# Attention's values: plain products first, and the other weight sums grown in four raw pages

## The chip, the cores and the metric

The kernel runs on one core of a Trainium2 chip. Its engines work side by side, each through its own instructions in order: TensorE (PE; its weight loads are PEld), VectorE (DVE), ScalarE (ACT), GpSimd (POOL) and SyncE (SP). Transfers run on 16 DMA engines that the core shares among its queues: SP and ACT issue plain transfers, POOL issues those that add to their destination, and some stores. The metric is the time of one execution on the device in microseconds (us).

## The reference, cut to what matters

One layer of a hybrid encoder for 512 tokens, model width 2048, in float32. The part that counts here is the first projection and its split:

```python
h = rms_norm(x, norm_mix_w[i])
proj = h @ w_in[i]
q_a, k_a, v_a, q_g, k_g, v_g, r_g, gate_lr = split_cols(proj, IN_SPLITS)
...
gate_logit = (gate_lr @ w_gla_gate_up[i] + b_gla_gate[i]).astype(jnp.float32)
log_a = (jax.nn.log_sigmoid(gate_logit) / GLA_GATE_TAU).reshape(B, T, GLA_HEADS, GLA_DK)
```

`v_a` (attention's values) and `v_g` (the values of gated linear attention) are 1024 columns each. The gate's logarithm is summed up along each chunk of 64 tokens (a scan) and used as exp(b) and exp(-b). Attention, gated linear attention, the output projection, a gated feed-forward block and a gated embedding follow.

## The kernel before, in words

Every product of matrices is made of float32r pieces: a weight page of 128 x 1024 is loaded raw, ACT copies it to a high part, VectorE subtracts that from the raw page and gives the low part ("split"), and three products of halves are added in PSUM. Each half has a ring of three buffers (tags h0 to h2 and l0 to l2), so the split of page n + 2 waits until PE has ended page n - 1.

The work goes in this order: `first_values` and `second_values` make the two halves of `v_g` with plain products, eight pages of 24 matmuls each; then comes attention's values; then the list of steps of all later projections, beginning with q and k of the four linear heads (units 12 to 15).

Attention's values are the product of two matrices cut in two both ways, with seven products of quarters in place of eight. The weights' quarters are L11, L12, L21 and L22, and the products P1 to P7 want L11, L12, S1 = L21 + L22, S2 = S1 + L11, S3 = L21 + L11, S4 = S2 + L12 and L22. The operand's quarters are R11, R21 and R22 and the differences N1, N2, T3 and T4. Each product takes four pages of 12 matmuls (128 x 512), so there are 28 pages, numbered 0 to 27 in the order of `VALUE_ORDER`. `values_product` loads page n + 4, splits page n + 2, runs what `plan` holds for page n and then gives page n to PE. `values_collect` brings a finished product from PSUM into one of four result quarters C11, C12, C21 and C22 (`VALUE_SLOTS`, halves of the x pages) and stores a finished quarter to DRAM (`vad`, L1173).

The sums of weights are made beforehand in DRAM: `value_chores` copies a page from DRAM to DRAM on SP's queue (L1113) and two chores later adds another to it on POOL's (L1116), for four pages of each of S1, S2, S4 and S3. The chores run between the pages of the gated values.

The x pages hold the layer's input in eight pairs of blocks (tags r3 to r7, u0, u1 and c0). `scale_pair(k)` applies the norm to pair k and makes R11's piece, `right(k)` makes those of R21 and R22, `differences(k)` replaces the pair by its four differences (four instructions of VectorE) and `spread_differences(k)` splits these into operand pieces named "h" (one instruction of ACT and one of VectorE). Pairs 2 to 7 get their differences between pages 4 and 14. The gate's steps are `gate_low` to `gate_ln`, `gate_sum`, `gate_scan`, `gate_decay` and `gate_small`; sums and scans run in the last pages of `second_values`.

`values_out` evicts a half of `v_g` from PSUM on ACT and stores it to DRAM (`vgd`, L277) from ACT's queue. `linear` loads it again (`load_v`, L1374, SP).

What sets the order: a scheduler may move instructions, except where an `InOrder` engine (`vec`, `act`, `ten`, `syn`) is switched on by `in_order`. From `second_values` on, ACT, VectorE and TensorE keep the order of the program text; SP does not, and POOL has no such wrapper. `give(tag)` returns a tag to the list of free pages and lets `issue` load weights of the coming steps into it.

## Time and profile before

| what | value |
|---|---|
| median of three runs | 2264.49 us (2262.75 to 2265.28) |
| the profiled execution's own time | 2269.32 us |
| its span | 2267.4 us |
| granted clock of TensorE over it | 0.995 |
| first matmul of attention's values | 104.36 us |
| first matmul of the steps after them | 199.65 us |

The profile is of one execution. Times in its views count from the start of the span. A row of the timeline has start, length, engine, line, operation and tiles, and in brackets the idle time of the engine ahead of it and what ended it; nearly all instructions stand under L64, the wrapper's line, so that they are told apart by their tiles: "wva_P_r" is a raw page of attention's values, "wva_h" and "wva_l" its halves, "vaA", "vaB" and "vaC" the PSUM banks, "h" the spread differences, "va_S" a sum in DRAM, "g_t" a tile of the gated part. A row of a group has its count, busy time and mean length; a row of waits has us in total, times and the longest. A row of stretches has the length, busy time and count for each engine, the granted clock, the DMA engines' share and GB/s.

### The profile page before, as it was taken

What the parts mean: (1) busy time and instruction counts of PE and PEld (TensorE: products, weight loads), DVE (VectorE), ACT (ScalarE), POOL (GpSimd) and SP (SyncE); (2) the same over time, 40 slices, a digit from 0 to 9 for tenths busy, and PEclk for the clock granted to TensorE, in tenths of its full rate; (3) what the DMA queues carried; (4) which work ended last, traced back from release to release, by engine and by line L of the source; (5) the groups of instructions that cost most, each with busy time, mean ns of one, the idle gap of its engine ahead of it and who ended that gap; (6) DMA issues with size and microseconds to landing.
All of it is one profiled execution on the core that took longest, in us unless ns stands there. A gap on an engine that the chain in (4) does not pass through costs nothing.

```text
span 2267.4 us, 45711 instructions
## 1 busy us (share of the span) xinstructions
PE 2240.1 (99%) x18248; PEld 2182.5 (96%) x18248; DVE 1893.6 (84%) x2599; ACT 1322.3 (58%) x1960; POOL 198.6 (9%) x243
## 2 busy tenths in 40 slices
PE   9989999999999999999999999999999999999997
PEld 8768999999999999999999999999999999999997
DVE  5775779998788888999888888888898787898987
ACT  6564567776575665555555555555564554666765
POOL 1101111010000001111111110000000100000000
PEclk9999999999999999999999999999999999999999
DMA  9967888887978979999999987877866967879896
GB/s 295 303 228 205 224 230 231 234 241 215 335 280 256 327 240 257 290 291 289 283 271 275 271 231 210 219 214 202 249 237 227 306 217 227 324 243 333 282 294 207
DMA packets 205830, 583.42 MB, mean 257 GB/s; under 512 B 22480, under 2 KB 64720, under 8 KB 205616
## 3 DMA queue, kind: packets, MB, share of 16 engines
q1 hardware_dynamic: 169680, 460.12, 56.9%
q0 software_dynamic: 32320, 115.88, 27.4%
q10 hardware_dynamic: 3616, 4.49, 0.6%
q8 instruction: 143, 2.34, 0.4%
q14 instruction: 71, 0.58, 0.1%
HBM read 507.01 MB, written 136.31 MB: 284 GB/s over the span
## 4 chain that ended last, share of the span: by engine, by line
PE 85%; DVE 6%; DMA 5%; ACT 2%; issue 2%; ACTq 0%; SPq 0%; DVEq 0%; POOLq 0%
PE accA L64 42%; PE accC L64 22%; PE accB L64 11%; PE v L64 3%; DVE wl L64 1%; PE vaA L64 1%; DMA on<-ond 1%; PE pp L64 1%; PE psc L64 1%; PE ptr L64 1%; PE py L64 1%; DMA wva_P_r<-in_w_v_a 1%; DMA s<-in_w_up 1%; DVE u L64 1%; DVE s L64 1%
## 5 line engine op out<-in xcount | busy, mean ns | idle before, releaser
L64 DVE TENSOR_TENSOR wl<-s,wh 128x1024 fp32r<-128x1024 f32 (+1 forms) x381 | 457.6, 1201 | 82.3 <-ACT wh L64 76.8
L64 ACT ACTIVATE wh<-l 128x1024 fp32r<-128x1024 f32 (+1 forms) x320 | 331.7, 1038 | 187.0 <-PE accC L64 119.4
L64 PE MATMUL accA<-h,wh 128*128 128x256 f32 x3392 | 433.8, 280 | 0.6 <-ACT u L64 0.5
L64 DVE TENSOR_TENSOR wl<-l,wh 128x1024 fp32r<-128x1024 f32 (+1 forms) x320 | 382.5, 1196 | 59.4 <-ACT wh L64 58.7
L64 ACT ACTIVATE wh<-s 128x1024 fp32r<-128x1024 f32 (+1 forms) x381 | 395.0, 1037 | 38.1 <-DVE s L64 21.7
L64 PEld LDWEIGHTS accA<-h,wh 128*128 128x128 f32 x3392 | 412.4, 188 | 3.2 <-ACT u L64 1.2
L64 PE MATMUL accC<-h,wh 128*128 128x256 f32 x2832 | 361.5, 279 | 0.3 <-ACT u L64 0.3
L64 PEld LDWEIGHTS accC<-h,wh 128*128 128x128 f32 x2832 | 343.8, 188 | 0.8 <-ACT u L64 0.5
L64 ACT ACTIVATE u<-accA 128x256 f32<-128x256 f32 x302 | 114.2, 378 | 381.5 <-PE accA L64 381.3
L64 PE MATMUL accA<-h,wl 128*128 128x256 f32 x1696 | 233.5, 279 | 0.7 <-DVE wl L64 0.7
L64 DVE TENSOR_TENSOR s<-s,l 128x1024 f32<-128x1024 f32 (+1 forms) x176 | 211.3, 1201 | 7.7 <-DMA s<-in_w_blk 4.2
L64 PEld LDWEIGHTS accA<-h,wl 128*128 128x128 f32 x1696 | 213.4, 188 | 0.9 <-DVE wl L64 0.9
L64 PE MATMUL accC<-h,wl 128*128 128x256 f32 x1416 | 195.2, 279 | 0.9 <-DVE wl L64 0.9
L64 PEld LDWEIGHTS accC<-h,wl 128*128 128x128 f32 x1416 | 178.3, 188 | 1.3 <-DVE wl L64 1.3
L442 POOL DMA_DIRECT2D s<-in_w_up x84 | 74.0, 880 | 738.5 <-DMA s<-in_w_up 284.1
L64 DVE SCALAR_TENSOR_TENSOR cv<-u,cw,cv 128x511 f32<-128x511 f32 (+1 forms) x176 | 131.7, 748 | 3.1
L64 ACT ACTIVATE u<-accC 128x256 f32<-128x256 f32 x98 | 37.4, 382 | 91.1 <-PE accC L64 90.7
L64 DVE TENSOR_TENSOR u<-u,accC 128x256 f32<-128x256 f32 x102 | 42.7, 418 | 56.8 <-PE accC L64 55.7
L64 PE MATMUL accA<-up_N,wh 128*128 128x256 f32 x704 | 89.5, 279 | 0.4 <-ACT u L64 0.4
L64 PE MATMUL accA<-up_R,wh 128*128 128x256 f32 x704 | 89.7, 280 | 0.0
L64 PE MATMUL accB<-up_R,wh 128*128 128x256 f32 x704 | 89.3, 279 | 0.0
L64 PEld LDWEIGHTS accA<-up_N,wh 128*128 128x128 f32 x704 | 85.2, 188 | 0.6 <-ACT u L64 0.6
(343 smaller groups left out, 3649.8 us busy)
## 6 DMA issues: line engine op xcount, KB each, us to landing
l<-in_w_up SPq DMA_DIRECT2D x132, 512.0 KB, 6.7
s<-in_w_up SPq DMA_DIRECT2D x84, 512.0 KB, 6.0
s<-in_w_up POOLq DMA_DIRECT2D x84, 512.0 KB, 7.6
l<-in_w_dn SPq DMA_DIRECT2D x56, 448.0 KB, 4.9
l<-in_w_blk SPq DMA_DIRECT2D x48, 512.0 KB, 5.3
s<-in_w_blk SPq DMA_DIRECT2D x32, 512.0 KB, 4.5
s<-in_w_blk POOLq DMA_DIRECT2D x32, 512.0 KB, 7.3
l<-in_w_out SPq DMA_DIRECT2D x28, 512.0 KB, 4.7
```

Of the source, the lines that this page charges most:

```text
L64: ins = f(*args, **kw)
L442: nc.gpsimd.dma_start(t, src("L22" if name == "S1" else "L11"), accum_op=ALU.add)
```

## The change

The sums are no longer made in DRAM: `value_chores` and its calls are gone. The products go in the order P1, P2, P4, P5, P6, P3, P7: first the three with plain weights. In the meantime four raw pages (tags r4, r5, r7 and u0) are loaded with L21 and get L22 added to them (S1, for P5); when a page has been split, L11 is added (S2, for P6), and after the next split L12 (S4, for P3). P7's four pages are loaded with L21 on the ordinary ring and get L11 added. All of these adds are accumulating DMAs from POOL into SBUF, tied to page numbers.

The operand work moves with it. Pairs 0 to 3 get their differences and spreads within `second_values` and pair 4 its differences there, the rest by page 9. Gate sums and scans move from `second_values` to pages 10 to 15, decays to 16 to 19. The second half of `v_g` is evicted in pages 0 and 1 instead of ahead of them. The stores of `v_g` move from ACT's queue to POOL's, and POOL gets a wrapper of its own; SP and POOL keep the order of the text within the stage. The vgd loads in `load_v` keep it too. C11 and C12 use one pair of result halves (slot 3), C22 and C21 slots 6 and 7; a fourth bank D is used; and P7 ends two quarters, C21 and C22.

```diff
-    def values_out(ps, c, tiles):
-        for t in range(TT):
+    def values_out(ps, c, tiles, ts=range(TT)):
+        for t in ts:
             act.activation(tiles[t], ps[t], AF.Copy, scale=rtok[:, t:t + 1])
-            nc.scalar.dma_start(vgd[2 * c:2 * c + 2, :, t].rearrange("h p v -> p h v"),
+            pool.dma_start(vgd[2 * c:2 * c + 2, :, t].rearrange("h p v -> p h v"),
...
-    VALUE_SLOTS = {"C11": 1, "C12": 4, "C22": 5, "C21": 7}
-    VALUE_ORDER = ("P1", "P2", "P3", "P6", "P5", "P7", "P4")
-    VALUE_BANKS = {"P1": "A", "P2": "B", "P3": "C", "P6": "A", "P5": "B", "P7": "A", "P4": "A"}
+    VALUE_SLOTS = {"C11": 3, "C12": 3, "C22": 6, "C21": 7}
+    VALUE_ORDER = ("P1", "P2", "P4", "P5", "P6", "P3", "P7")
+    VALUE_BANKS = {"P1": "A", "P2": "B", "P4": "D", "P5": "C", "P6": "A", "P3": "C", "P7": "A"}
+    SUM_TAGS = ("r4", "r5", "r7", "u0")
...
     def value_load(v, n):
-        if n < len(v["pages"]):
-            prod, j = v["pages"][n]
-            raw = v["raw"][n] = page("wr", f"wva_{prod}{j}_r")
-            syn.dma_start(raw, value_page(PRODUCTS[prod][0], j))
+        prod, j = v["pages"][n]
+        raw = v["raw"][n] = page("wr", f"wva_{prod}{j}_r")
+        syn.dma_start(raw, value_page("L21" if prod == "P7" else PRODUCTS[prod][0], j))
+
+    def sum_load(v, j):
+        raw = v["sum"][j] = pg.tile([P, 1024], F32, tag=SUM_TAGS[j], name=f"wva_s{j}")
+        syn.dma_start(raw, value_page("L21", j))
+
+    def sum_more(v, n, name):
+        prod, j = v["pages"][n]
+        raw = v["raw"][n] if prod == "P7" else v["sum"][j]
+        v["raw"][n] = raw
+        pool.dma_start(raw, value_page(name, j), accum_op=ALU.add)
...
-        todo = {0: [(gate_low,), (scale_pair, 2)],
-                1: [(scale_pair, 3), (right, 0), (right, 1)],
+        todo = {0: [(gate_low,), (scale_pair, 2), (right, 0)],
+                1: [(scale_pair, 3), (differences, 0), (right, 1)],
                 2: [(gate_up,), (gate_abs, (0, 1)), (scale_pair, 4), (gate_min, (0, 1))],
                 3: [(gate_abs, (2, 3)), (scale_pair, 5), (gate_min, (2, 3)), (right, 2)],
-                4: [(gate_exp, (0, 1, 2, 3)), (scale_pair, 6), (differences, 0)],
-                5: [(gate_ln, (0, 1, 2, 3)), (scale_pair, 7), (gate_sum, (0, 1))],
-                6: [(gate_sum, (2, 3)), (gate_scan, (0, 1))],
-                7: [(gate_scan, (2, 3)), (spread_differences, 0)]}
+                4: [(gate_exp, (0, 1, 2, 3)), (scale_pair, 6), (differences, 1), (right, 3)],
+                5: [(gate_ln, (0, 1, 2, 3)), (scale_pair, 7), (differences, 2)],
+                6: [(spread_differences, 0), (differences, 3), (spread_differences, 1)],
+                7: [(spread_differences, 2), (spread_differences, 3), (right, 4), (differences, 4)]}
...
+    for n, *fs in ((0, (second_out, (0, 1)), (spread_differences, 4)),
+                   (1, (second_out, (2, 3)), (sum_load, va, 0), (right, 5), (right, 6)), (2, (differences, 5)),
+                   (3, (sum_load, va, 1), (spread_differences, 5)), (4, (right, 7), (sum_more, va, 12, "L22")),
+                   (5, (sum_load, va, 2), (differences, 6)), (6, (sum_more, va, 13, "L22"), (spread_differences, 6)),
+                   (7, (sum_load, va, 3), (differences, 7)), (8, (sum_more, va, 14, "L22")),
+                   (9, (sum_more, va, 15, "L22"), (spread_differences, 7)), (10, (gate_sum, (0, 1))), (11, (gate_scan, (0,))),
+                   (12, (gate_sum, (2, 3))), (13, (gate_scan, (1,))), (14, (gate_scan, (2,))), (15, (gate_scan, (3,))),
+                   *((11 + j, (sum_more, va, 16 + j, "L11"), (value_load, va, 24 + j)) for j in range(4)),
+                   *((15 + j, (sum_more, va, 20 + j, "L12")) for j in range(4)),
+                   *((18 + j, (sum_more, va, 24 + j, "L11")) for j in range(4)),
+                   *((16 + i, (gate_decay, (i,))) for i in range(4)),
+                   *((20 + i, (gate_small, (i,))) for i in range(4)), (26, (linear_pages,)),
+                   *((n, (give, tag)) for n, tag in ((19, "r4"), (20, "r5"), (23, "r1"), (24, "r2"), (25, "r0"), (26, "r3")))):
```

More of the change, by code (lines that the diff above doesn't have):

```diff
@@ L70, in encoder_block @@
     vec, act, ten = InOrder(nc.vector), InOrder(nc.scalar), InOrder(nc.tensor)
-    syn = InOrder(nc.sync)
+    syn, pool = InOrder(nc.sync), InOrder(nc.gpsimd)
     def in_order(on, loads=False):
@@ L76, in in_order @@
             e.on = on
-        syn.on = loads
+        syn.on = pool.on = loads
     ident = cp.tile([P, P], F32, name="ident")
@@ L247, in first_values @@
             if kp == 4:
-                chores.extend(value_chores())
                 gate_weights()
@@ L436, in issue @@
             if name[0] == "L":
-                nc.sync.dma_start(t, src(name))
+                syn.dma_start(t, src(name))
             elif unit.sums == "memory":
@@ L440, in issue @@
             else:
-                nc.sync.dma_start(t, src("L21"))
-                nc.gpsimd.dma_start(t, src("L22" if name == "S1" else "L11"), accum_op=ALU.add)
+                syn.dma_start(t, src("L21"))
+                pool.dma_start(t, src("L22" if name == "S1" else "L11"), accum_op=ALU.add)
     sumd = {}
@@ L1095, in norm_root @@
         norm["w"] = rstd_begin(norm["ms"])
-    value_sums, plan = {}, {}
+    plan = {}
+    VALUE_SLOTS = {"C11": 3, "C12": 3, "C22": 6, "C21": 7}
+    VALUE_ORDER = ("P1", "P2", "P4", "P5", "P6", "P3", "P7")
+    VALUE_BANKS = {"P1": "A", "P2": "B", "P4": "D", "P5": "C", "P6": "A", "P3": "C", "P7": "A"}
+    SUM_TAGS = ("r4", "r5", "r7", "u0")
     def value_page(name, j):
-        if name[0] == "S":
-            return value_sums[name, j]
         return A["w_v_a"][int(name[1]) - 1, 4 * (int(name[2]) - 1) + j]
-    def value_chores():
-        todo = [(name, j) for name in ("S1", "S2", "S4", "S3") for j in range(4)]
-        first = {"S1": "L21", "S2": "L11", "S3": "L21", "S4": "L12"}
-        second = {"S1": "L22", "S2": "S1", "S3": "L11", "S4": "S2"}
-        def chore(i):
-            if i < len(todo):
-                name, j = todo[i]
-                value_sums[name, j] = scratch(f"va_{name}{j}", (P, 1152))[:, :1024]
-                tc.keep_in_program_order(nc.sync.dma_start(value_sums[name, j], value_page(first[name], j)))
-            if 2 <= i < len(todo) + 2:
-                name, j = todo[i - 2]
-                tc.keep_in_program_order(nc.gpsimd.dma_start(value_sums[name, j], value_page(second[name], j),
-                                                             accum_op=ALU.add))
-        return [lambda i=i: chore(i) for i in range(len(todo) + 2)]
@@ L1139, in values_product @@
         acc2 = v["ps"][VALUE_BANKS[prod]]
-        fresh = prod in ("P1", "P2", "P3", "P5")
+        fresh = prod in ("P1", "P2", "P4", "P5")
         for j in range(4):
             n = 4 * VALUE_ORDER.index(prod) + j
-            value_load(v, n + 4)
+            if n + 4 < 12:
+                value_load(v, n + 4)
             value_split(v, n + 2)
@@ L1161, in values_collect @@
         acc2 = v["ps"][VALUE_BANKS[prod]]
-        parts = {"P1": (("C11", 1, 0),), "P2": (("C11", 1, 1),), "P3": (("C12", 1, 0),), "P6": (("C12", 1, 0),),
-                 "P5": (("C22", -1, 0), ("C12", 1, 1)), "P7": (("C22", -1, 1),), "P4": (("C21", -1, 1),)}[prod]
+        parts = {"P1": (("C11", 1, 0),), "P2": (("C11", 1, 1),), "P4": (("C21", -1, 0),), "P5": (("C22", -1, 0),),
+                 "P6": (("C12", 1, 0),), "P3": (("C12", 1, 1),), "P7": (("C21", -1, 1), ("C22", -1, 1))}[prod]
         for quarter, sign, done in parts:
@@ L1172, in values_collect @@
                 if done:
-                    nc.gpsimd.dma_start(vad[4 * c:4 * c + 4, :, 2 * h + i].rearrange("b p v -> p b v"),
+                    pool.dma_start(vad[4 * c:4 * c + 4, :, 2 * h + i].rearrange("b p v -> p b v"),
                                         dst.rearrange("p (b v) -> p b v", b=4))
@@ L1330, in split_page @@
                 value_split(va, k - KD // 2)
-            for _ in range(2 if 2 <= k < 6 else 1):
-                if chores:
-                    chores.pop(0)()
-        todo = {0: [(gate_low,), (scale_pair, 2)],
-                1: [(scale_pair, 3), (right, 0), (right, 1)],
+        todo = {0: [(gate_low,), (scale_pair, 2), (right, 0)],
+                1: [(scale_pair, 3), (differences, 0), (right, 1)],
                 2: [(gate_up,), (gate_abs, (0, 1)), (scale_pair, 4), (gate_min, (0, 1))],
                 3: [(gate_abs, (2, 3)), (scale_pair, 5), (gate_min, (2, 3)), (right, 2)],
-                4: [(gate_exp, (0, 1, 2, 3)), (scale_pair, 6), (differences, 0)],
-                5: [(gate_ln, (0, 1, 2, 3)), (scale_pair, 7), (gate_sum, (0, 1))],
-                6: [(gate_sum, (2, 3)), (gate_scan, (0, 1))],
-                7: [(gate_scan, (2, 3)), (spread_differences, 0)]}
+                4: [(gate_exp, (0, 1, 2, 3)), (scale_pair, 6), (differences, 1), (right, 3)],
+                5: [(gate_ln, (0, 1, 2, 3)), (scale_pair, 7), (differences, 2)],
+                6: [(spread_differences, 0), (differences, 3), (spread_differences, 1)],
+                7: [(spread_differences, 2), (spread_differences, 3), (right, 4), (differences, 4)]}
         for k in range(3):
@@ L1358, in second_values @@
             values_page(ps, *tiles.pop(k), k)
-        values_out(ps, 1, [gt("t8"), gt("t9"), gt("S", 768)[:, :T], gt("t10")])
+        va["first"] = ps
     def linear(unit):
@@ L1373, in load_v @@
             for i in range(2):
-                nc.sync.dma_start(M["V"][i], vgd[h][:, 2 * i:2 * i + 2])
+                tc.keep_in_program_order(nc.sync.dma_start(M["V"][i], vgd[h][:, 2 * i:2 * i + 2]))
         def keys():
@@ L1488, in linear_pages @@
         G["s"] = pg.tile([P, 2, T], F32R, tag="r7", name="squares")
+    va = dict(pages=[(p, j) for p in VALUE_ORDER for j in range(4)], raw={}, sum={}, tiles={}, have=set())
     def at_page(n, *fs):
@@ L1495, in give @@
         issue()
-    for n, *fs in ((0, (differences, 1)), (1, (spread_differences, 1)), (2, (right, 3), (right, 4)), (3, (right, 5), (right, 6)),
-                   (4, (right, 7)), *((4 + 2 * i - (i == 5), (differences, 2 + i)) for i in range(6)),
-                   *((5 + 2 * i - (i == 5), (spread_differences, 2 + i)) for i in range(6)),
-                   *((3 + 2 * i, (gate_decay, (i,))) for i in range(4)),
-                   *((15 + i, (gate_small, (i,))) for i in range(4)), (24, (linear_pages,)),
-                   *((n, (give, tag)) for n, tag in ((16, "r5"), (18, "r4"), (23, "r1"), (24, "r2"), (25, "r0"), (26, "r3")))):
+    out_tiles = []
@@ new lines, in second_out @@
+    def second_out(ts):
+        if not out_tiles:
+            out_tiles.extend((gt("t8"), gt("t9"), gt("S", 768)[:, :T], tp.tile([P, T], F32, tag="sq", name="v_out")))
+        values_out(va["first"], 1, out_tiles, ts)
+    for n, *fs in ((0, (second_out, (0, 1)), (spread_differences, 4)),
[11 more added lines that the diff above has]
+                   *((n, (give, tag)) for n, tag in ((19, "r4"), (20, "r5"), (23, "r1"), (24, "r2"), (25, "r0"), (26, "r3")))):
@@ L1503, in encoder_block @@
         at_page(n, *(lambda f=f, a=a: f(*a) for f, *a in fs))
-    va = dict(pages=[(p, j) for p in VALUE_ORDER for j in range(4)], raw={}, tiles={}, have=set())
     first_values(A["w_v_g"])
     second_values(A["w_v_g"])
-    va["ps"] = {b: [(psum_mm if b == "C" else psum_aux)(f"va{b}{i}") for i in range(2)] for b in "ABC"}
+    in_order(True, True)
+    va["ps"] = {b: [(psum_mm if b in "CD" else psum_aux)(f"va{b}{i}") for i in range(2)] for b in "ABDC"}
     for p in VALUE_ORDER:
         values_product(va, p)
-        if p == "P4":
+        if p == VALUE_ORDER[-1]:
@@ L1514, in encoder_block @@
         values_collect(va, p)
+    in_order(True)
     pctx.close()
```

## The prediction

> **What bounds the kernel now.** I read the page first, for the kernel as a whole.

> ```profile
> span 2267.4 us, 45711 instructions
> PE 2240.1 (99%) x18248; PEld 2182.5 (96%) x18248; DVE 1893.6 (84%) x2599; ACT 1322.3 (58%) x1960; POOL 198.6 (9%) x243
> q1 hardware_dynamic: 169680, 460.12, 56.9%
> q0 software_dynamic: 32320, 115.88, 27.4%
> ```

> TensorE is busy nearly throughout, so only a stage in which it waits, or runs below its clock, can pay. The second reading is busy time by stage: the second half of the gated values (59.86 to 104.36), attention's values (104.36 to 199.65, the stage of this change), the first products after it; and two short stretches inside the stage.

> ```profile
> 59.86:104.36 44.50, 44.50 (x197) 36.79 (x196) 32.49 (x48) 23.40 (x35) 7.31 (x9) 1.00 1.04 309
> 104.36:199.65 95.29, 86.69 (x337) 65.00 (x336) 68.02 (x93) 51.90 (x66) 7.83 (x10) 0.95 0.74 227
> 110.00:118.00 8.00, 5.49 (x14) 3.38 (x13) 3.50 (x6) 2.81 (x3) 0.00 (x0) 0.79 0.89 282
> 162.00:168.00 6.00, 6.00 (x15) 4.69 (x16) 3.98 (x10) 1.06 (x1) 0.00 (x0) 0.52 0.64 188
> 199.65:220.00 20.35, 20.35 (x176) 20.34 (x175) 9.66 (x11) 9.22 (x13) 3.31 (x4) 1.00 0.79 230
> ```

> The columns are length, then PE, PEld, DVE, ACT and POOL busy, the granted clock, the DMA engines' share and GB/s. Before and after the stage PE is full at clock 1.00. Inside it is idle 95.29 - 86.69 = 8.6 us, at a mean clock of 0.95; the loss of clock sits behind the stalls (0.79 in 110 to 118, 0.52 in 162 to 168). VectorE has 68 of 95 us, so it is no bound over the stage as a whole.

> Third, the pitch of an undisturbed page: the eviction of each page's high part starts when a page of products has ended, so two neighbours at the end of the stage show it.

> ```profile
> 179.72 1.06 ACT L64 ACTIVATE wva_h<-wva_P_r 128x1024 fp32r<-128x1024 f32 x1 [1.25 <-PE vaA L64]
> 182.52 1.06 ACT L64 ACTIVATE wva_h<-wva_P_r 128x1024 fp32r<-128x1024 f32 x1 [1.74 <-PE vaA L64]
> ```

> 182.52 - 179.72 = 2.80 us a page; 28 pages need 78.4 us. The stage takes 95.29, so **16.9 us** is all there is to win in it: 8.6 idle, the rest lost clock and short gaps.

> Fourth, who ends PE's waits in the stage.

> ```profile
> PE vaA L64 <- DVE h L64: 2.7, 2, 2.2
> PE vaA L64 <- DVE wva_l L64: 1.9, 3, 0.8
> PE vaA L64 <- ACT wva_h L64: 1.6, 2, 1.1
> PE vaB L64 <- DVE wva_l L64: 1.1, 2, 0.8
> PE vaC L64 <- DVE wva_l L64: 0.9, 2, 0.5
> ```

> Two causes stand behind these rows. The weight pages came late, and ACT, in order, was late behind them; and the operand pieces that VectorE spreads ("h") came one by one between the pages' own splits, the last at 160.50, with PE standing for it.

> ```profile
> ACT wva_h L64 <- DMA wva_P_r<-in_w_v_a: 14.5, 3, 5.6
> 96.98 1.06 ACT L64 ACTIVATE wva_h<-wva_P_r 128x1024 fp32r<-128x1024 f32 x1 [3.87 <-DMA wva_P_r<-in_w_v_a]
> 103.61 1.06 ACT L64 ACTIVATE wva_h<-wva_P_r 128x1024 fp32r<-128x1024 f32 x1 [5.57 <-DMA wva_P_r<-in_w_v_a]
> 106.23 0.37 ACTq L277 DMA_DIRECT2D vgd<-g_t  x1
> SPq L1374 <- DMA vgd<-g_t: 8.0, 2, 7.1
> 159.50 0.73 PE L64 MATMUL vaA<-wva_h,h 128*128 128x512 f32 x2 [2.15 <-DVE h L64]
> 160.50 1.22 DVE L64 TENSOR_TENSOR h<-pair_c,h 128x1024 fp32r<-128x1024 f32 x1
> ```

> **The change, part by part.** Write T(n) for the start of page n; T(0) = 104.36, pages 2.80 apart if nothing stalls. Durations, back to back, from groups of the stage and single rows:

> ```profile
> L64 DVE TENSOR_TENSOR wva_l<-wva_P_r,wva_h 128x1024 fp32r<-128x1024 f32 x27 | 33.0, 1223 | 25.2 <-ACT wva_h L64 25.2
> L64 ACT ACTIVATE wva_h<-wva_P_r 128x1024 fp32r<-128x1024 f32 x27 | 28.0, 1053 | 30.4 <-DMA wva_P_r<-in_w_v_a 10.6 <-PE vaA L64 8.7 <-PE vaB L64 7.0
> 112.34 0.88 DVE L64 TENSOR_TENSOR pair_r<-pair_r 128x256 f32<-128x256 f32 x2
> 113.26 0.88 DVE L64 SCALAR_TENSOR_TENSOR pair_r<-pair_r 128x256 f32<-128x256 f32 x2
> 100.42 2.33 DVE L64 TENSOR_TENSOR_SCAN g_t<-g_t,g_t 128x512 f32<-128x512 f32 x2
> 93.49 1.29 DVE L64 TENSOR_TENSOR g_t<-g_t,g_t 128x512 f32<-128x512 f32 x2
> 120.74 1.29 DVE L64 TENSOR_TENSOR in_R<-pair_r,in_R 128x512 fp32r<-128x512 f32 x2
> L64 DVE TENSOR_TENSOR pair_r<-pair_r,vaB 128x512 f32<-128x512 f32 x4 | 2.7, 684 | 0.4 <-ACT pair_u L64 0.4
> 105.53 0.67 ACT L64 ACTIVATE g_t<-v,rtok 128x512 f32<-128x512 f32 x1
> 106.64 0.69 ACT L64 ACTIVATE g_t<-v,rtok 128x512 f32<-128x512 f32 x1 [0.44 <-ACT g_t L64]
> ```

> So a split costs ACT 1.05 and VectorE 1.22; differences 2 x 0.88 = 1.76; a scan 1.17; a gate sum or a "right" piece 0.65; an add of results 0.68; a spread piece as much as a split.

> *Sums out of DRAM.* 16 DRAM-to-DRAM copies (SP) and 16 DRAM accumulates (POOL) go, and of 28 page loads 12 plain ones, four sum loads and four for P7 stay: 24 fewer issues on SP. POOL keeps 16 accumulates, now into SBUF and between the page's uses. This frees the DMA engines before T(0), where their share is 1.04: the pages that ACT got at 96.98 and 103.61 were issued at 79.75 and 85.19, 17 and 18 us before; at the pace of the stage a load takes 4.2. I cost the loads of P1, P2 and P4 at nothing, behind two pages of lead.

> ```profile
> 79.75 0.33 SPq L64 DMA_DIRECT2D wva_P_r<-in_w_v_a  x1
> 85.19 0.33 SPq L64 DMA_DIRECT2D wva_P_r<-in_w_v_a  x1
> wva_P_r<-in_w_v_a SPq DMA_DIRECT2D x8, 512.0 KB, 4.2
> L442 POOL DMA_DIRECT2D s<-in_w_blk x32: 851/877/1418, 189.0 to 575.4; - x32
> DMA to landing us min/median/max: 5.1/7.8/15.4
> 196.49 1.22 DVE L64 TENSOR_TENSOR s<-s,l 128x1024 f32<-128x1024 f32 x1
> ```

> *Stores.* The four stores of the second half of gated values stood on ACT's queue between evictions; from one eviction to the next went 106.64 - 105.53 = 1.1 us, and 0.67 without the store; all eight go to POOL (0.88 us an issue), on which nothing else waits then. The evictions themselves now follow the splits of pages 2 and 3 instead of going ahead of page 2's. The vgd loads of the first linear unit leave SP's queue in the stage, where SP stood 8.0 us for them; they now follow in their place, as the later units' do.

> *Differences and spreads earlier.* Four differences (7.0), four spreads (4.9) and two "right" pieces (1.4) now lie ahead of T(0), two scans (2.3) and four sums (2.6) leave. VectorE there: 32.5 + 13.3 - 4.9 + the second page's split 1.2 = 42.1 of 44.5 us. It fits; only the last of the eight pages (about 6 us against 5.5) runs over. In the stage VectorE has 28 splits (34.2), four spreads (4.9), three differences (5.3), three "right" (2.0), sums and scans (2.6 + 4.7), small decays and four adds of results (4.3): 58 of 78.4. Page by page the sums are at most 2.9 us of 2.8 (pages 2, 5, 7), and neighbours are lighter. A page's high part may start two pages before its use, at T(n), and both halves are done by T(n) + 2.3; they are wanted at T(n) + 5.6, so 3.3 us of queueing are free. Put down in their order, ACT and VectorE come closest at page 6, where a late spread and P1's two copies hold ACT to T(4) + 1.7 (both halves done at + 3.9, wanted at + 5.6), and at page 10, where P2's two adds hold VectorE to T(8) + 2.8 (done at + 4.0). At least 1.6 us are left, so the cost is zero; without that cover each page would stall by what it lacks.

> *The four growing pages.* This is the unknown price. Page 12 + j is split by T(10+j) + 2.3; then its accumulate may issue, lands L later, and page 16 + j needs 2.3 more and is wanted at T(16+j). So L may be 16.8 - 4.6 = 12.2 us. L of all such accumulates is 5.1 / 7.8 / 15.4 (smallest, median, largest), so at the median 4.4 us remain. On POOL's queue the accumulates for pages 14 and 15 stand behind the stores of C11, which wait for VectorE's adds after T(8); they issue near T(8) + 3.5 and 4.3, 11 and 13 us before their splits must begin (T(14) - 2.3 and T(15) - 2.3): more than 7.8.

> The DMA engines bound L. From the page, a 0.524 MB accumulate holds all 16 for 0.524 / (115.88 / (0.274 x 2267.4)) = 2.8 us, a load 0.524 / (460.12 / (0.569 x 2267.4)) = 1.5. Between T(8) and T(24), 44.8 us, stand 14 accumulates (39.3), four loads (5.9) and two 256 KB stores (2.8): 48.0, and at the share of 1.04 that the row before the stage reached, 46.6 fit. The engines are then full, 1.4 to 3.2 us over. Nothing (the 4.4 us cover it) and 6.4 (3.2 idle, and as much again at half clock) are the ends of the bill; I take 2.0 (1.0 idle, 1.0 of clock), nearer nothing, because the last four (P7's) were never urgent: issued from about T(17) + 3, wanted from T(22).

> *The end of the stage.* P7 ends with four adds on VectorE (2.7 us) instead of two ACT copies; the next split that PE wants is due at T(28) + 5.6. The first linear unit's S1 page comes free at T(22) + 2.3, loads (4.2) and accumulates (7.8): T(22) + 14.3, and its sum (1.22) and split (2.3) must be begun by T(28) + 2.1 = T(22) + 18.9. Covered by 4.6; without that cover PE would wait for the rest in the first product that uses it.

> *Sum.* Profiled time 2269.3 (span 2267.4) - 16.9 + 2.0 = 2254.4. The median of the runs, 2264.5, lies 4.8 under that execution, so 2249.6.

> *The clock.* The rows of 110 to 118 have PE idle for 2.5 us in gaps of at most 1.1 us, and a clock of 0.79; so I let a stall cost its length again. [...]

> **The rivals.**
> *Faster, but the chain of sums is late.* L near 12 to 14 while loads of the next stage share the engines; PE then waits at P6, P3 or P7. For it: the engines are full. Against: the stage's own loads are over by then. Price 5 to 11 in place of 2.0: 2252.6 to 2258.6.
> *Slower.* One mechanism, the sums' loop. If L stays at 15.4 or more, page 16 waits 15.4 - 12.2 = 3.2, and in P3, whose pages now start late, each round takes 15.4 + 2.3 instead of 11.2, 6.5 more: 9.7 idle, and with half clock after each of the two (162 to 168, at 0.52, loses 2.9 us) 15.5, nearly all of the gain of 16.9. Beyond about 16 it is slower: at 18, 5.8 + 9.1 + 5.8 = 20.7, 2268.3. Against: 15.4 is the largest that this line shows.
> *No change.* The stalls were the split order's, not the loads', and come back at pages 0 to 3, where ACT has over 3 us a page (split, two evictions, a spread) and VectorE enters late: 1 us a page over the first 14 and clock loss, about 2264.

> **How the numbers follow.** As forecast 0.62 (2245.5 to 2254.5), late chain 0.20, no change 0.06, slower 0.12. A measurement of this kernel can tell about 0.2%, 4.5 us. Faster 0.82, same 0.06, slower 0.12. The range 2245.5 to 2262 leaves out the slower case and little else.

> **What would show it.** Right: no wait of PE for "h" or "wva_h" in the stage, granted clock 1.00 from 104 on, the stage near 80 us, evictions 2.80 apart, wva pages landed in 4 to 6 us. The price of the chain: PE or ACT waiting for the DMA into "wva_s", and the landing times of POOL's accumulates against 12.2. Wrong: gaps that begin at page 16 and repeat every four pages, a granted clock of a half behind them, or a first product after the stage that waits for its S1.

## The result and the profile after

The changed kernel takes 2252.22 us (median of 4 runs, 2250.46 to 2254.96), the kernel before 2264.89 beside it: a ratio of 0.9941, 95% interval 0.9920 to 0.9963. Two later series of 5 runs each gave 2254.17 and 2252.47, with the kernel before at 2264.96 and 2264.35 (ratios 0.9955 and 0.9946). It is 11 to 13 us faster; 15 were forecast. The profiled execution took 2254.96 (span 2253.2); the sum had 2254.4 for it.

The page of the kernel after:

```profile
span 2253.2 us, 45669 instructions
PE 2230.6 (99%) x18248; PEld 2178.5 (97%) x18248; DVE 1892.1 (84%) x2599; ACT 1321.7 (59%) x1960; POOL 205.8 (9%) x251
q1 hardware_dynamic: 166224, 447.54, 55.7%
q0 software_dynamic: 32960, 117.98, 27.5%
```

Busy time by stage (length, PE, PEld, DVE, ACT, POOL, granted clock, DMA share, GB/s), with the second half of the gated values, attention's values and the first steps after them:

```profile
59.50:104.00 44.50, 44.50 (x198) 36.79 (x197) 37.80 (x59) 27.80 (x40) 0.00 (x0) 1.00 0.31 108
104.00:184.56 80.56, 79.46 (x337) 62.88 (x336) 56.28 (x75) 47.25 (x60) 21.98 (x26) 1.00 0.98 254
184.56:220.00 35.44, 31.94 (x272) 31.31 (x271) 24.81 (x29) 13.79 (x18) 5.32 (x7) 1.00 0.89 257
```

The stage went from 95.29 to 80.56 us, at full clock. Ahead of it the DMA engines' share fell from 1.04 to 0.31; now the stage itself has them full, at 0.98. The third row is new: PE stands 3.5 us *after* the stage, where before it lost 0.2. Who ended PE's waits from 104 to 220, and ACT's from 104 to 200:

```profile
PE accB L64 <- DVE wl L64: 1.8, 1, 1.8
PE pat L64 <- DVE g_t L64: 1.7, 1, 1.7
PE vaA L64 <- DVE wva_l L64: 0.8, 1, 0.8
PE vaA L64 <- ACT wva_h L64: 0.2, 1, 0.2
```

```profile
ACT wva_h L64 <- DMA wva_P_r<-in_w_v_a: 17.3, 6, 4.1
ACT wva_h L64 <- DMA wva_s<-in_w_v_a: 7.0, 5, 1.9
```

No wait for "h" is left, and the products ahead of P7 cost PE nothing: all their pages, and P7's first, start 2.80 us after the one before. The two small waits in the stage stand at P7's pages (174.3 and 175.6), the last three of which come 3.1, 3.9 and 3.1 us after the one before. ACT's timeline there (start, length, operation, idle time ahead and its releaser) shows them as they land:

```profile
161.90 2.14 ACT L64 ACTIVATE wva_h<-wva_s 128x1024 fp32r<-128x1024 f32 x2
168.15 1.06 ACT L64 ACTIVATE wva_h<-wva_P_r 128x1024 fp32r<-128x1024 f32 x1 [4.10 <-DMA wva_P_r<-in_w_v_a]
173.22 1.06 ACT L64 ACTIVATE wva_h<-wva_P_r 128x1024 fp32r<-128x1024 f32 x1 [4.01 <-DMA wva_P_r<-in_w_v_a]
176.36 1.06 ACT L64 ACTIVATE wva_h<-wva_P_r 128x1024 fp32r<-128x1024 f32 x1 [2.08 <-DMA wva_P_r<-in_w_v_a]
179.52 1.06 ACT L64 ACTIVATE wva_h<-wva_P_r 128x1024 fp32r<-128x1024 f32 x1 [2.10 <-DMA wva_P_r<-in_w_v_a]
```

Their four accumulates were issued from 157.4 to 159.0, so they took 10.7 to 20.4 us to land, twice as long as the twelve into the growing pages (groups of DMA issues from 104 to 200: count, KB each, median us to landing):

```profile
wva_s<-in_w_v_a POOLq DMA_DIRECT2D x12, 512.0 KB, 8.3
wva_P_r<-in_w_v_a POOLq DMA_DIRECT2D x4, 512.0 KB, 16.5
```

The late pages also explain the waits after the stage. The first linear unit's S1 page is the page that P7's first split frees (170.47). From there the timeline of SP, POOL and VectorE runs so:

```profile
170.49 5.40 SPq L64 DMA_DIRECT2D s<-in_w_blk  x2
178.72 0.86 POOL L64 DMA_DIRECT2D s<-in_w_blk  x1 [17.48 <-DVE wva_l L64]
185.63 1.23 DVE L64 TENSOR_TENSOR s<-s,l 128x1024 f32<-128x1024 f32 x1 [2.65 <-DMA s<-in_w_blk]
208.39 1.23 DVE L64 TENSOR_TENSOR s<-s,l 128x1024 f32<-128x1024 f32 x1 [6.40 <-DMA s<-in_w_blk]
```

S1 is complete at 185.6. PE still bridges that, but this unit's pages come free late, so the next unit's S1 lands at 208.3, and VectorE, in order, stands 6.4 us for it with two low parts and the gate's work queued behind: those are PE's waits of 1.8 and 1.7.

### The profile page after: what moved, and what is told of

Read it like the earlier page. It is cut to its first block, busy times and chain, and to the rows that moved or that the text cites. A ratio compares the mean times of both kernels' runs of the same rounds, so it can differ in the third digit from the quotient of the medians.

```text
span 2253.2 us, 45669 instructions
## 1 busy us (share of the span) xinstructions
PE 2230.6 (99%) x18248; PEld 2178.5 (97%) x18248; DVE 1892.1 (84%) x2599; ACT 1321.7 (59%) x1960; POOL 205.8 (9%) x251
## 4 chain that ended last, share of the span: by engine, by line
PE 82%; DVE 4%; DMA 2%; ACT 1%; issue 1%; DVEq 0%; SPq 0%; ACTq 0%
PE accA L64 44%; PE accC L64 22%; PE accB L64 11%; DVE wl L64 1%; PE pp L64 1%; PE py L64 1%; PE psc L64 1%; PE ptr L64 1%; DVE u L64 1%; PE po L64 1%; DVE s L64 1%; DVE xs L64 0%; DMA on<-ond 0%; DMA x3d<-xs 0%; DMA s<-in_w_ple_gate 0%
## 5 line engine op out<-in xcount | busy, mean ns | idle before, releaser
L64 DVE TENSOR_TENSOR wl<-s,wh 128x1024 fp32r<-128x1024 f32 (+1 forms) x381 | 457.4, 1201 | 77.3 <-ACT wh L64 70.2
L64 ACT ACTIVATE wh<-l 128x1024 fp32r<-128x1024 f32 (+1 forms) x320 | 331.7, 1038 | 183.2 <-PE accC L64 119.1
L64 PE MATMUL accA<-h,wh 128*128 128x256 f32 x3392 | 433.7, 280 | 0.6 <-ACT u L64 0.5
L64 DVE TENSOR_TENSOR wl<-l,wh 128x1024 fp32r<-128x1024 f32 (+1 forms) x320 | 382.5, 1195 | 57.2 <-ACT wh L64 56.4
L64 ACT ACTIVATE wh<-s 128x1024 fp32r<-128x1024 f32 (+1 forms) x381 | 394.7, 1036 | 42.3 <-DVE s L64 27.5
L64 PEld LDWEIGHTS accA<-h,wh 128*128 128x128 f32 x3392 | 411.8, 188 | 3.2 <-ACT u L64 1.2
L64 PE MATMUL accC<-h,wh 128*128 128x256 f32 x2832 | 361.4, 280 | 0.5 <-ACT u L64 0.5
L64 PEld LDWEIGHTS accC<-h,wh 128*128 128x128 f32 x2832 | 343.2, 188 | 0.9 <-ACT u L64 0.7
L64 ACT ACTIVATE u<-accA 128x256 f32<-128x256 f32 x302 | 114.3, 379 | 382.1 <-PE accA L64 381.9
L64 PE MATMUL accA<-h,wl 128*128 128x256 f32 x1696 | 233.5, 279 | 0.7 <-DVE wl L64 0.7
L64 DVE TENSOR_TENSOR s<-s,l 128x1024 f32<-128x1024 f32 (+1 forms) x176 | 211.2, 1200 | 10.2 <-DMA s<-in_w_blk 10.2
L64 PEld LDWEIGHTS accA<-h,wl 128*128 128x128 f32 x1696 | 213.0, 188 | 0.9 <-DVE wl L64 0.9
L64 PE MATMUL accC<-h,wl 128*128 128x256 f32 x1416 | 195.0, 279 | 0.3 <-DVE wl L64 0.3
L64 PEld LDWEIGHTS accC<-h,wl 128*128 128x128 f32 x1416 | 177.8, 188 | 0.5 <-DVE wl L64 0.5
L64 POOL DMA_DIRECT2D s<-in_w_up x84 | 74.0, 881 | 734.5 <-DMA s<-in_w_up 393.0
L64 DVE SCALAR_TENSOR_TENSOR cv<-u,cw,cv 128x511 f32<-128x511 f32 (+1 forms) x176 | 131.6, 748 | 3.1
L64 DVE TENSOR_TENSOR u<-u,accC 128x256 f32<-128x256 f32 x102 | 42.6, 418 | 57.9 <-PE accC L64 57.0
L64 ACT ACTIVATE u<-accC 128x256 f32<-128x256 f32 x98 | 37.4, 382 | 91.3 <-PE accC L64 90.9
L64 PE MATMUL accA<-up_R,wh 128*128 128x256 f32 x704 | 89.8, 280 | 0.0
L64 PE MATMUL accB<-up_R,wh 128*128 128x256 f32 x704 | 89.4, 279 | 0.0
L64 PE MATMUL accA<-up_N,wh 128*128 128x256 f32 x704 | 89.4, 279 | 0.0
L64 PEld LDWEIGHTS accA<-up_R,wh 128*128 128x128 f32 x704 | 85.2, 188 | 0.5 <-issue 0.5
## 6 DMA issues: line engine op xcount, KB each, us to landing
l<-in_w_up SPq DMA_DIRECT2D x132, 512.0 KB, 6.5
s<-in_w_up SPq DMA_DIRECT2D x84, 512.0 KB, 5.9
s<-in_w_up POOLq DMA_DIRECT2D x84, 512.0 KB, 7.6
l<-in_w_blk SPq DMA_DIRECT2D x48, 512.0 KB, 5.5
s<-in_w_blk SPq DMA_DIRECT2D x32, 512.0 KB, 4.7
s<-in_w_blk POOLq DMA_DIRECT2D x32, 512.0 KB, 7.8
l<-in_w_out SPq DMA_DIRECT2D x28, 512.0 KB, 4.6
```

The lines of the kernel that those rows point to most:

```text
L64: ins = f(*args, **kw)
```

## The experiments

In each, "before" and "after" are the two kernels above; times are medians, with the kernel before run beside them.

### The two causes, each alone and both (before at 2265.12, 12 runs)

*No sums made (b_nosum).*

```diff
-                chores.extend(value_chores())
...
         if name[0] == "S":
-            return value_sums[name, j]
+            name = {"S1": "L21", "S2": "L11", "S3": "L21", "S4": "L12"}[name]
```

> The kernel before, with the 16 copies and 16 adds in DRAM left out and a plain weight page of the same size loaded in place of each sum (so four of the seven products use wrong weights); the order of all other work is as before. Two causes (late weight pages at the start of the stage, and late operand pieces "h" later in it): the half clock at 113 us and the waits for wva_h and wva_l go, the waits for "h" (2.7 us in three) and the 6.8 us of half clock near 161 (3.4 us lost) stay, so 9 to 12 us below before, 2253 to 2256. Rival, loads alone (the "h" pieces are late only because the splits ahead of them waited for pages): 16 to 17 us below, about 2248. Rival, order alone: within 2 us of before.

Measured: 2258.93 (2257.16 to 2261.64, 8 runs), ratio 0.9972 (0.9961 to 0.9982): 6.2 us faster. PE's waits in the stage, and the stage:

```profile
PE vaA L64 <- DVE h L64: 2.5, 2, 2.2
PE vaB L64 <- DVE wva_l L64: 1.2, 2, 0.8
PE vaC L64 <- DVE wva_l L64: 0.9, 2, 0.5
```

```profile
104.25:193.20 88.95, 83.04 (x337) 62.75 (x336) 63.86 (x90) 49.49 (x62) 7.13 (x9) 0.98 0.71 220
```

The half clock at 113 is gone (one stretch at 0.50 is left, from 155.92 to 159.34), the waits for "h" stay, as the theory of two causes has it. But the waits for "wva_l" stay too: those splits were late on VectorE, behind differences and spreads, and not for want of a page. So the pages are worth 6, not 9 to 12.

*The order alone (b_order).* The kernel before, sums still in DRAM.

```diff
-                4: [(gate_exp, (0, 1, 2, 3)), (scale_pair, 6), (differences, 0)],
...
-                7: [(gate_scan, (2, 3)), (spread_differences, 0)]}
+                4: [(gate_exp, (0, 1, 2, 3)), (scale_pair, 6), (differences, 1), (right, 3)],
...
+                7: [(spread_differences, 2), (spread_differences, 3), (right, 4), (differences, 4)]}
...
-    for n, *fs in ((0, (differences, 1)), (1, (spread_differences, 1)), (2, (right, 3), (right, 4)), (3, (right, 5), (right, 6)),
+    for n, *fs in ((0, (spread_differences, 4)), (1, (right, 5), (right, 6)), (2, (differences, 5)),
+                   (3, (spread_differences, 5)), (4, (right, 7)), (5, (differences, 6)), (6, (spread_differences, 6)),
+                   (7, (differences, 7)), (9, (spread_differences, 7)), (10, (gate_sum, (0, 1))), (11, (gate_scan, (0,))),
```

> The kernel before, with the sums still made in DRAM, but with differences, spreads, right pieces, gate sums, scans and decays on the pages where the changed kernel has them. Two causes: the waits for "h" and the half clock near 161 go, the late pages and the half clock at 113 stay: 4 to 7 us below before, 2258 to 2261. Rival, loads alone: within 2 us of before. Rival, order alone: 14 to 17 us below, about 2249.

Measured: 2257.93 (2256.66 to 2258.69, 5 runs), ratio 0.9968 (0.9955 to 0.9981): 7.2 us faster. What is left is the late page and the half clock behind it (0.50 from 113.48 to 120.31):

```profile
PE vaA L64 <- ACT wva_h L64: 3.4, 1, 3.4
PE vaA L64 <- DVE pair_u L64: 0.6, 1, 0.6
PE vaA L64 <- DVE wva_l L64: 0.6, 1, 0.6
```

*Both (b_both).* The two edits together.

> Both of these edits in one: no sums made at all (four products with wrong weights), and the order of operand work of the changed kernel. Two causes: the stage runs at its pitch, 79 us, 16 to 17 us below before, about 2248; what the changed kernel takes above this (some 4 us) is the bill of its growing pages. Rival (the in-order queues and stores of the change carry part of the gain): 10 to 13 us below before, no better than the changed kernel, 2252.

Measured: 2250.83 (2248.03 to 2253.61, 4 runs), ratio 0.9938 (0.9923 to 0.9953): 14.3 us faster, and 6.2 + 7.2 = 13.4 by the parts. The stage takes 79.27 us, as expected; the 16 to 17 us were reckoned from the prediction's 95.29, which the last run below puts 2.2 too high. So the two causes add up to the whole gain. This kernel has neither the stores on POOL nor the in-order queues of the change; a_nop7, the next run, has both and took 2250.69, so what they carry is too small for these runs to see.

### The bill of the growing pages

*Without P7's accumulates (a_nop7).* Run beside the three above.

```diff
-                   *((18 + j, (sum_more, va, 24 + j, "L11")) for j in range(4)),
```

> The changed kernel without the four accumulates for P7's pages (P7 then uses L21 in place of L21 + L11). The theory: these four, last in a full queue, are the whole remaining bill: ACT's waits for P7's pages go (PE idle 0.9 near 174) and, since P7's first page comes free on time, the first linear unit's S1 too (PE idle 1.8 and 1.7 near 209 and 216): 3.5 to 4.6 us below the changed kernel, 2247.6 to 2248.7. Rival (that unit's sum is late by its own load, add and queue, whatever P7 does): about 1 us below, 2251.

Measured: 2250.69 (2249.25 to 2251.87, 4 runs), ratio 0.9939 (0.9922 to 0.9955). The stage and the steps after it:

```profile
104.38:182.77 78.39, 78.39 (x337) 63.17 (x336) 58.94 (x78) 47.37 (x60) 18.93 (x23) 1.00 0.92 249
182.77:220.00 37.23, 37.23 (x317) 36.88 (x316) 25.48 (x31) 16.30 (x21) 7.36 (x9) 1.00 0.84 252
```

PE stands nowhere: 78.39 us is the pitch of 2.80 times 28. Nothing but these four transfers was left out, so in the profiles they carry all of PE's waits, in the stage and after it: the next unit's S1 is in place on time. The times say less. The profiled execution is 4.1 to 5.3 us below those of the changed kernel, but the median is 1.5 us below the first series and 1.8 and 3.5 below the two later ones, taken on other chips. The 3.5 to 4.6 that was expected is therefore seen in the profiles and not resolved by the medians, and the first series alone would fit the rival of about 1 us.

```profile
172.52 0.86 POOL L64 DMA_DIRECT2D s<-in_w_blk  x1 [14.47 <-DVE pair_r L64]
201.93 1.23 DVE L64 TENSOR_TENSOR s<-s,l 128x1024 f32<-128x1024 f32 x1 [1.73 <-DMA s<-in_w_blk]
```

*The changed kernel again (after2), P7's accumulates earlier (a_p7first), two loads later (a_late_l).* The kernel before took 2264.96 beside these and the next.

> The changed kernel once more, as it is, for more runs and a second profile. The theory (the stall near 209 and 216 follows from P7's first page landing late): 2250 to 2255 in single runs, median 2252, and in the second profile the two waits of 1.8 and 1.7 us are as long as P7's first accumulate is late against about 165.5 (the split that PE and the next S1 page wait for). Rival (those waits belong to the one execution): P7's pages late again and no wait near 209 and 216.

Measured: 2254.17 (2252.96 to 2258.70, 5 runs). The wait near 214 is there again with P7's pages as late, the one near 209 is not, so the two are not simply as long as P7's first page is late (it landed at 169.1, 1.1 us later than in the first profile):

```profile
PE pat L64 <- DVE g_t L64: 1.7, 1, 1.7
PE vaA L64 <- DVE wva_l L64: 1.5, 2, 0.8
PE accA L64 <- DVE wl L64: 0.4, 1, 0.4
```

For a_p7first the accumulates of P7 go between those for P6 and those for P3:

```diff
+                   *((14 + j, (sum_more, va, 24 + j, "L11")) for j in range(4)),
                    *((15 + j, (sum_more, va, 20 + j, "L12")) for j in range(4)),
-                   *((18 + j, (sum_more, va, 24 + j, "L11")) for j in range(4)),
```

> P7's four accumulates put on POOL's queue between those for P6 and those for P3 (pages 14 to 17 in place of 18 to 21). The theory (engines full from 116 to 176, so whatever stands last is late by the same backlog, and the last must be what has most time): P3's pages land up to four accumulates later, 8 to 10 us, with 2 to 3 us to spare: PE waits 5 to 8 us in P3, 2257 to 2261. Rival (P7's were late by their place in the queue only): the wait at P7 and after it goes and none comes, 2249.

Measured: 2261.59 (2259.09 to 2263.84, 11 runs), ratio 0.9982 (0.9973 to 0.9991): 7.4 us slower than the changed kernel beside it, two thirds of the gain, and just above the range that was expected. The waits in P3 are those that were forecast, 5.6 us; the half clock behind two of them was not. PE's waits from 104 to 215, and two stretches behind which the clock fell (each followed by one at half clock):

```profile
PE vaC L64 <- ACT wva_h L64: 3.8, 2, 2.2
PE vaC L64 <- DVE wva_l L64: 1.8, 3, 0.8
```

```profile
160.52:163.93 3.41, 1.30 (x4) 0.86 (x5) 1.22 (x1) 2.31 (x4) 0.00 (x0) 1.00 1.07 211
163.93:167.34 3.41, 3.41 (x9) 2.63 (x8) 0.58 (x1) 1.67 (x3) 0.00 (x0) 0.50 1.06 226
170.76:174.17 3.41, 0.62 (x2) 0.19 (x1) 1.08 (x1) 1.06 (x1) 0.00 (x0) 1.00 0.99 264
174.17:177.58 3.41, 3.21 (x8) 2.54 (x9) 1.16 (x5) 1.80 (x2) 0.00 (x0) 0.50 0.10 28
```

The engines are full (1.07) until all sums are made, and then nearly idle (0.10). The backlog is the same; put on P3's pages, it stops PE in the stage, and the half clock comes on top. Of the two places tried, last in the queue is the better one for P7.

For a_late_l, inside the last line of the list of pages:

```diff
- ... (give, tag)) for n, tag in ((19, "r4"), (20, "r5"), ...
+ ... (give, tag)) for n, tag in ((23, "r4"), (23, "r5"), ...
```

> The changed kernel with pages r4 and r5 given to the next stage at page 23 in place of 19 and 20, so that the two 512 KB loads of L11 and L12 no longer run beside P7's accumulates. The theory: two loads of 1.3 to 1.5 us go from ahead of P7's pages, which land 1.3 to 3 us earlier, and the wait near 174 and part of the later two goes: 1 to 3 us below the changed kernel if L11 and L12 are still in time (wanted near 180, landing near 175 to 178), else PE waits for them instead. Rival (an accumulate is slow by itself there): P7's pages 3 to 5 us apart as before, no change.

Measured: 2252.43 (2252.24 to 2253.77, 5 runs), 1.7 us below the changed kernel beside it. The edit did not move the two loads: they were issued at 158.75 and 160.99, against 158.80 and 161.03 in the changed kernel, since what they wait for is the split that frees the page, and no other transfer stands ahead of them on SP's queue. So it does not test the theory, although its numbers look like it: P7's pages landed 1.1 to 2.5 us earlier than in the first profile, the stage took 78.78 us, and 2.9 us of waits stood after it. By its issue times this is another repeat of the changed kernel, and then P7's lateness differs by that much between executions; no run here shows whether the edit acts in some other way.

*P7's sums on VectorE (a_p7vec).*

```diff
-                   *((18 + j, (sum_more, va, 24 + j, "L11")) for j in range(4)),
+                   *((18 + j, (other_load, va, j)) for j in range(4)),
+                   *((21 + j, (other_add, va, 24 + j)) for j in range(4)),
...
+    def other_load(v, j):
+        raw = v["other"][j] = pg.tile([P, 1024], F32, tag=SUM_TAGS[j], name=f"wva_o{j}")
+        syn.dma_start(raw, value_page("L11", j))
+
+    def other_add(v, n):
+        raw = v["raw"][n]
+        vec.tensor_tensor(raw, raw, v["other"][n - 24], ALU.add)
```

> P7's sums made by a plain load of L11 into each growing page after its last use and one add on VectorE, in place of the accumulate; the pages r4 and r5 are given to the next stage three pages later. The theory (the engines' time is the bill: an accumulate takes 2.45 to 2.8 us of all 16 engines, a load 1.3 to 1.5, so 4 to 5 us fewer up to P7): no wait in P7 and none near 209 to 217, 1.5 to 3.5 us below the changed kernel, 2248.5 to 2250.5. Rival (queues, not engine time): the late L11 and L12 of the first linear unit make PE wait instead, 2252 or more.

Measured: 2252.22 (2251.64 to 2255.07, 5 runs), ratio 0.9941 (0.9928 to 0.9955). PE's waits from 104 to 220:

```profile
PE pat L64 <- DVE g_t L64: 1.7, 1, 1.7
PE accB L64 <- DVE wl L64: 0.9, 1, 0.9
PE vaA L64 <- DVE wva_l L64: 0.5, 1, 0.5
```

The stage is at 79.22, 0.8 over its pitch, but the waits after it stay: the S1 load now stands on SP's queue behind a load of L12 that waits for VectorE's second add, and its accumulate is issued only at 176.85, 6.5 us ahead of the stage's end; a_nop7 has 10.3. Half of the forecast holds; S1's place in the queue, for the other half, is what the next runs try. The time is 1.95 us below the changed kernel beside it, which the two intervals (after2: 0.9942 to 0.9968) do not resolve.

### S1 first

Beside these runs the changed kernel (after3) took 2252.47 (2251.46 to 2254.60, 5 runs), and the kernel before 2264.35.

> The changed kernel once more, on the chip of the next two runs, to compare them with. By its runs so far 2252 to 2254 in the median; PE's wait of 1.69 us for g_t near 214 is there again.

Both held: PE's wait for g_t is 1.7 us again.

*P7's sums on VectorE and S1 ahead of L11 (a_p7vec2); S1 ahead alone (a_s1first).* The diff on top of a_p7vec, or of the changed kernel:

```diff
     def give(tag):
+        if tag == "r4":
...
+            wanted.insert(0, wanted.pop(2))
         free.append(tag)
```

In a_s1first r4 and r5 are also given at page 22 in place of 19 and 20; in a_late_l such a move left the issue times as they were.

> P7's sums on VectorE as before, and the first linear unit's S1 takes the first free page (r4) in place of its L11, so that its load and its accumulate start about 5 us sooner. The theory (the wait near 208 to 217 is the tail of that unit's S1: its accumulate was issued 10.3 us ahead of the stage's end in the run without P7's accumulates, which waited nowhere, 5.8 ahead in the changed kernel and 6.5 with P7's sums on VectorE): issued near 172 to 173, 10 us ahead, no wait of PE from 104 to 220, and 2250 to 2251, 2 to 3 us below the changed kernel. Rival (L11 and L12, now later, are awaited instead): a wait of 1 to 3 us near 180, 2252 or more.

Measured: 2250.29 (2246.75 to 2254.28, 6 runs), ratio 0.9934 (0.9922 to 0.9946). S1's accumulate was issued at 173.11, 10.2 us ahead of the stage's end, and PE's waits from 104 to 300 fell to 1.0 us:

```profile
PE pat L64 <- DVE g_t L64: 0.5, 1, 0.5
PE vaA L64 <- DVE wva_l L64: 0.5, 1, 0.5
```

Of the kernels that leave no work out it is the fastest here, 2.2 us below the changed kernel beside it. The two intervals (after3: 0.9935 to 0.9958) overlap, so the difference is seen in the waits and not resolved by the times. The two edits together leave 0.5 us of PE's waits after the stage; with a_p7vec alone there were 2.6, and with the next run's edit alone 1.6.

> The changed kernel with that order of the first linear unit's loads alone; P7's accumulates stay. By the theory S1's accumulate, behind P7's four in a full queue, lands near 182 in place of 185.5, and the waits for wl and g_t after the stage shrink from 3.5 to 0 to 1.5 us; P7's own wait of 0.8 to 1.5 stays: 1.5 to 3 us below the changed kernel. If the engines' load alone counts and S1 only pushes something else back, no change.

Measured: 2253.73 (2249.61 to 2254.43, 5 runs), ratio 0.9944 (0.9932 to 0.9956). Against after3, S1's accumulate was issued 9.4 us earlier, at 170.26, and landed 2.6 earlier, at 183.09; PE's wait after the stage was 1.57 in place of 1.95. No gain in time, as the second expectation had it: it stands behind P7's on the queue, and took 12.8 us to land.

### The kernel before once more

> The kernel before once more, for a second profile. The sum of the prediction took the stage's 16.9 us from an execution 4.8 us above the median and took those 4.8 as lying outside the stage. If so, the stage is 95 us long again. If part of them lay in the stage, it is 91 to 94 us here and fewer than two stretches of half clock stand in it.

Measured: 2264.78, with this stage:

```profile
104.39:197.44 93.05, 84.77 (x338) 64.30 (x336) 67.94 (x93) 51.68 (x66) 7.82 (x10) 0.96 0.75 233
```

2.24 us shorter than in the execution the prediction was made from, with two stretches of half clock as there, but of 3.41 us each (from 118.64 and from 159.59) in place of 3.41 and 6.83. So part of the 4.8 lay in the stage, as the second guess had it, though not by fewer stretches of half clock.

## Why the prediction was right, and where it was off

*The two causes* were right, and each was shown alone: 6.2 and 7.2 us, 14.3 together. The split between them was not part of the forecast; that late "wva_l" belongs to VectorE's order was learned from the first experiment.

*The rival of no change* (the stalls were the split order's alone) fell: the order alone gives half. *Costs put at nothing* held for stores, differences, spreads and the adds of results: with a_nop7 the stage runs at its pitch with nothing late. VectorE ahead of the stage took 37.8 us where I counted 42.1.

*"So 16.9 us is all there is to win"* was right for that one execution (78.39 was reached) and mis-sized for the median. I took 16.9 from an execution 4.8 above the median and then took the 4.8 off once more, as if it lay elsewhere. The second profile has 93.05 in the stage, 14.7 to win: about 2.2 of the 4.8 lay in the stage itself. The kernel without P7's accumulates, which pays no bill, shows the same in the times: 2250.69, 3.1 above the 2247.6 that the sum gives with a bill of nothing.

*The bill of 2.0* stood for stalls in the stage, and there its size held, by some luck: three profiles of the changed kernel have the stage at 80.45 to 80.63, 2.1 to 2.2 over the pitch, all of it at P7's pages and at full clock, where I had taken 1.0 idle and 1.0 of lost clock. The growing pages themselves (P6, P3), where I had looked for the bill, cost nothing; L there was 6.0 to 10.6 against the 12.2 allowed. What did not hold is that P7's last four "were never urgent: issued from about T(17) + 3, wanted from T(22)". They were issued at T(17) + 5.8 (157.4) and on, took 10.7 to 20.4 us, where I had counted on a median of 7.8, and ACT was ready for the first at 164.05, T(21) + 1.2.

The count of engine time behind it was short. Between T(8) and T(24) I put four plain loads (5.9). SP's queue moved 4.21 MB there (126.4 to 171.2 in the profile after), as much as eight of 0.524: loads still open at T(8), and L11 and L12 of the next stage, issued at 158.80 and 161.03. At the prediction's 1.5 us a load the four more are 6 us, an estimate; the last of the 14 accumulates landed at 179.42, 8.2 us after T(24) = 171.2. No run took these loads alone away.

The waits after the stage, put at nothing, are the part of the bill that was missed: 2.0 to 3.5 us in these three profiles, 4.1 to 5.7 in all, inside the ends of 0 and 6.4 (a_late_l has 0.4 and 2.9, 3.3 in all). In the medians, against a_nop7, the bill is 1.5 to 3.5. So the saving was 2.2 too high and the bill, by the profiles, 1.3 to 3.7 too low; the medians lie 2.6 to 4.6 above the forecast. That the profiled execution came within 0.6 of its sum was partly luck: the bill was 5.7 in it, 3.7 more than taken, and the rest of the kernel, by 2067.75 and 2068.68 us with 0.2 and 3.5 of waits, was 2.4 shorter by something that no run here explains.

*The end of the stage* was "covered by 4.6". S1 was complete 5.6 us later than counted: its page came free at 170.47 in place of 167.9 (2.6), its load took 7.7 in place of 4.2 (3.5), the wait for POOL 0.5, the accumulate 6.8 in place of 7.8. The mechanism was named; that the price would be paid a unit later, and not in the first product that uses the page, was not seen.

*The rival of the late chain* named P6, P3 or P7 and 5 to 11 us. Its mechanism came in part, at P7, with a price about its lowest: 3.3 to 5.7 by the profiles. Two medians (2252.2 and 2252.5) lie just below its lower end of 2252.6 and one (2254.2) inside it, and since the forecast's own band reaches to 2254.5, the times alone do not part the two. *The slower rival* did not come, though a_p7first shows it was near: with four more accumulates ahead of P3's pages, 7.4 of the 10.8 us won beside it were gone.

*The clock.* I let a stall cost its length again; in the three profiles of the changed kernel it cost only itself, with a granted clock of 1.00 in the stage and around the wait after it. The last section has the rows in which it cost more. *A sign of being right that failed* is "wva pages landed in 4 to 6 us": the ten plain loads of the ordinary ring in the stage took 4.4 to 10.0 (median 7.9), and PE waited for none of them.

## What to carry to other kernels

Before you move transfers out of a stage that they crowd (a share of 1.04 there, 0.31 afterwards), see whether the engines have room where they go (here they came to 0.98, and 4.1 to 5.7 us of the saving went back): count every transfer that runs there, the ones still open at its start and the next stage's among them, look for what is last in the new queue, and follow the page it holds to its next user, because the stall can appear a stage later, as 2.0 to 3.5 us of it did here. A saving read from one execution has to be set against that execution; before taking a distance to the median off, ask how much of it lies in the very stage that is to be saved. When the last transfers of a full queue are late, try taking work off the engines as well as reordering: here reordering moved the stall (5.6 us of waits in P3 with a_p7first), and a plain load and an add on an engine that had time shortened it (0.5 us at P7 in a_p7vec and a_p7vec2, against 1.0 to 1.5 in the changed kernel).

## What the runs showed of the hardware

```profile
109.75:113.16 3.41, 1.55 (x6) 0.78 (x5) 1.92 (x3) 1.06 (x1) 0.00 (x0) 1.00 1.01 264
113.16:116.57 3.41, 3.41 (x10) 2.42 (x8) 0.91 (x3) 0.33 (x1) 0.00 (x0) 0.50 1.00 371
157.54:160.95 3.41, 1.45 (x6) 1.05 (x6) 3.38 (x5) 2.01 (x2) 0.00 (x0) 1.00 0.52 154
160.95:167.77 6.82, 6.28 (x15) 4.74 (x15) 5.03 (x11) 1.06 (x1) 0.00 (x0) 0.50 0.60 168
```

The 3.41 us around PE's wait near 214, and those behind it, in the changed kernel, where the clock stayed at 1.00, and in a_p7vec, where it went to 0.50:

```profile
214.03:217.44 3.41, 1.72 (x15) 1.49 (x14) 3.41 (x6) 1.78 (x3) 0.00 (x0) 1.00 0.89 247
217.44:220.86 3.42, 3.42 (x33) 3.23 (x33) 2.64 (x4) 0.14 (x1) 0.00 (x0) 1.00 1.00 356
```

```profile
212.81:216.22 3.41, 1.72 (x17) 1.36 (x16) 3.02 (x4) 1.77 (x3) 0.00 (x0) 1.00 0.88 281
216.22:219.63 3.41, 3.41 (x20) 3.29 (x18) 2.17 (x3) 0.00 (x0) 0.67 (x1) 0.50 0.76 288
```

Up to 220 us, nine such falls were measured. In the 3.41 us ahead of eight of them TensorE was busy for 0.12 (b_order), 0.62 and 1.30 (a_p7first), 0.69 and 1.25 (before2), 1.26 (b_nosum), 1.45 and 1.55 us (before), and ahead of the ninth, in a_p7vec, for 1.72. Behind stretches with 1.71 (after2), 1.72 and 1.78 (the changed kernel), 2.07 (a_late_l) and 2.24 us (after3) it stayed at 1.00. So the wait of 1.7 us for g_t cost only itself in the changed kernel, and a stretch of half clock besides in a_p7vec. In the first row of the kernel before, no single gap was longer than 1.10 us. Of the eight falls inside the stage, six lasted 3.41 us, with TensorE busy for 3.06 us of it or more, and two (before and b_order) 6.82 and 6.83, with 6.28 in each.

*An accumulating transfer and full engines.* From 150 to 155 us POOL's accumulates were all that the engines moved (1.06 MB), and the changed kernel moved 211 GB/s at a share of 1.07:

```profile
150.00:155.00 5.00, 5.00 (x23) 4.05 (x22) 2.71 (x3) 4.45 (x7) 1.72 (x2) 1.00 1.07 211
```

By this row, as an estimate, one accumulate of 0.524 MB takes 0.524 / 211 GB/s = 2.5 us, and 2.7 us of engine time at that share, near the 2.8 that the prediction took from the page's averages. The weight pages loaded ahead of the stage, with the engines at 0.31, landed in 3.4 us, where before they took 17 to 18:

```profile
wva_P_r<-in_w_v_a SPq DMA_DIRECT2D x6, 512.0 KB, 3.4
```
